# A two-layer hybrid attention encoder on one core: another order of each layer's projections, other waits between the planner's lines

## The chip, the cores and the metric

The kernel runs on one core of a Trainium2 chip. The time is the device time of one execution in microseconds (us). A core has five engines that run their own instruction streams and wait for each other by semaphores: TensorE (PE, matmuls; PEld is its loading of the stationary operand), VectorE (DVE), ScalarE (ACT), GpSimd (POOL) and SyncE (SP, which here only issues DMA transfers). DMA transfers can also be issued from ACT's and POOL's instruction streams. A line number such as L241 is one of the kernel before.

## What is computed

Two layers, each one RMSNorm, one wide input projection, two kinds of attention side by side, gates, an output projection and a residual add; then a final RMSNorm. The sequence has 512 positions, the model 1024 features, all in float32.

```python
for layer in range(DEPTH):                               # 2
    h = rms_norm(x, norm_g[layer])
    p = h @ w_in[layer]
    c_q, c_kv, k_r, gate_a, dil_qkv, gate_b = jnp.split(p, split_points, axis=-1)
    a = mla_attention(c_q, c_kv, k_r, q_norm_g[layer], kv_norm_g[layer],
                      w_uq[layer], w_ukv[layer], cos_m, sin_m) * jax.nn.silu(gate_a)
    b = dilated_attention(dil_qkv, cos_d, sin_d) * jax.nn.silu(gate_b)
    x = x + jnp.concatenate([a, b], axis=-1) @ w_out[layer]
return rms_norm(x, final_g)
```

`mla_attention` is latent attention: queries, keys and values of 8 heads come from two normed low-rank latents (`c_q` with 384 features, `c_kv` with 256), and a shared rotated key joins them. `dilated_attention` has three groups of 8 heads of width 64 with windows (128, 512, 2048) and key strides (1, 4, 16); the three groups' outputs are mixed per position by their softmax denominators.

## The kernel before

Every float32 operand is kept as a high and a low half (`hl`, `whl` and so on), and every product is three matmuls into one PSUM bank, high by high, high by low and low by high (`triple`, L241 to L243). A weight tile is loaded by SP into `wraw`; ACT rounds it to the high half (L198); the low half is either a VectorE subtraction (L203) or, for the kinds in `ADDED` that come after place `FROM` in the plan, a negation by ACT (L200) and an adding DMA from POOL's queue (L201).

The order of the work is not written out. Each piece is a generator task. One main line holds a layer's projections in the order of the table `ORDER` and behind them the output projection (`wp`, `wq`, `wo` in layer 0, `wa` to `wj` in layer 1). The names in `ORDER`: `ckv` and `cq` the two latents, `v` the values of the wide windows, `nv` those of the narrow window, `mv` and `muk` the latent attention's values and keys, `muq` and `mur` its queries and their rotated part, `kr` the shared key, `dqk u 0` and `dqk u 1` the queries and keys of window unit u (12 units of two heads, numbered so that four pairs of heads go through the three windows), `ga` and `gb` the gates of the two branches. Beside the main line run side lines, each strictly in its own order: `nline` (norms: `norm`, `lckv`, `lcq`), `sline` (scores), `tline` (outputs, named `o`) and `cline` (combining and gating: `mo` gates a pair of latent heads, `do1` mixes the three windows of a pair, `do` gates them). `Weave` walks the main line with a clock of its own and lets a side task start when all it needs was done a given lag earlier; only when the main line is blocked by a need are side tasks forced ahead of their lags. The lags of before are LAG 2.5 for norms and combining, LM 2.0 for latent scores, LD 8.25 (LD0 10.0 for the first) for window scores, LG 6.0 and LG2 16.5 for outputs behind their scores. A side task is placed in the order of its line, so a late task holds up those behind it on its line. What comes out is then given to a tile scheduler and to pools with fixed numbers of buffers: 8 PSUM banks, 4 `whl`, 14 `hl`, 2 `xl`, 8 `p`, 5 `v`, 5 `tmp`.

The places that the steps below touch:

- **Start** (L286 to L298): ACT's queue issues the first weight tile, the norm factors `gn` (L289) and the second weight tile; SP's queue the inputs and the other six tiles. PE runs WARM matmuls on zeros (L296). Each input tile is scaled by `gn` and split (`take_x`, L273 and L274) and enters the first latent products (L376).
- **Query latent**: each chunk is squared (L350) and the squares are added by POOL (L354 for `cq`); PE turns the sum (L256), and the norm factor goes into every query (L491).
- **Rotated queries** `mla_rope`: L497 on VectorE, L498 on POOL, L499 and L500 on VectorE, a split; `mla_query` copies them into each head's `q` on POOL (L512). The latent scores are L241 to L243 on `kml` and `q`, with the maximum on VectorE (L525).
- **Window scores**: narrow window L673 with L680 on VectorE, wide windows L744 and L747 with L750 and L753. **Outputs**: probabilities are turned by PE (L449), split by ACT and VectorE (L221, L222) and multiplied by the values: L550 for latent heads, L785 for wide windows. L785 gives four banks a unit, each summed by ACT (L788) and VectorE (L789, L791).
- **Mixing** `combine`: PE turns the shares (L819), ACT copies them (L821), SP writes them to DRAM (L822) and reads them back spread over partitions by four transfers (L827); VectorE scales two windows' outputs (L831), POOL adds them (L832). `combine_last` adds the third on VectorE (L837), gates (L433) and splits (L221, L222).
- **Output projection** of layer 0: each 128 features of the next x are one bank; `out_add` loads x (L844), adds (L845), writes the sum to DRAM (L846) and hands it on to the next layer's `take_x`, through two `xl` buffers. Layer 1 ends with the final norm (L913 to L926) and the output writes.

A window score task of before waits for the unit's values as well as for its queries and keys:

```python
att.append((i, ("d", u), [k("dqk", u, 0), k("dqk", u, 1), k("v", g, p // 2) if g else k("nv", p)],
            far_scores if g else near_scores, far_out if g else near_out))
```

Of the kernel before, what the change touches and what calls it, by code (L numbers as in the profile page):

```python
# [22 lines left out]
AHEAD, RATE, LAG, CAP = 3, 451.1, 2.5, 34.9  # L23
STEP, LD0, WARM, LG2, LY = 2, 10.0, 11, 16.5, 5.0
LV = 3.0
LG, LP, LD, LM, LC, LN, LX, LF = 6.0, 0.25, 8.25, 2.0, 14.25, 5.75, 5.0, 0.25
SHUF = [i + 8 if i < 8 else i - 8 if i < 16 else i for i in range(32)]

def forward_order():
    return [('ckv',), ('v', 1, 0), ('cq', 2), ('cq', 0), ('cq', 1), ('dqk', 0, 0), ('dqk', 0, 1), ('nv', 0), ('mur', 0), ('ga', 0), ('dqk', 1, 0), ('kr',), ('dqk', 1, 1), ('nv', 1), ('muq', 0), ('muk', 0), ('mv', 0), ('muq', 1), ('dqk', 2, 1), ('muk', 1), ('dqk', 2, 0), ('muq', 2), ('dqk', 3, 1), ('muq', 3), ('dqk', 3, 0), ('dqk', 4, 1), ('mur', 1), ('v', 2, 0), ('muq', 4), ('dqk', 4, 0), ('dqk', 5, 0), ('muk', 2), ('ga', 1), ('muq', 5), ('dqk', 5, 1), ('mv', 1), ('dqk', 6, 0), ('nv', 2), ('gb', 0), ('muq', 6), ('dqk', 6, 1), ('muq', 7), ('nv', 3), ('dqk', 8, 0), ('gb', 1), ('muk', 3), ('v', 1, 1), ('ga', 2), ('dqk', 7, 0), ('dqk', 7, 1), ('dqk', 10, 0), ('dqk', 8, 1), ('dqk', 9, 0), ('dqk', 9, 1), ('v', 2, 1), ('dqk', 10, 1), ('ga', 3), ('dqk', 11, 0), ('dqk', 11, 1), ('gb', 2), ('gb', 3)]  # L30


def unit(u):

    return u % 6 // 2, 2 * (u // 6) + u % 2
# [20 lines left out]
PLAN = PLANS[0]  # L56
ADDED = ("dqk", "nv", "ga", "gb")
FROM = PLAN.index(("dqk", 0, 1, 1))
# [79 lines left out]
def hybrid_encoder(ctx, tc, xT, wst, gains, fgain, tables, keytab, masks, out):  # L138
    nc = tc.nc
# [35 lines left out]
    gn = const.tile([128, 2 * NG], F32, name="gn")  # L175
# [112 lines left out]
    load_w(nc.scalar, 0)  # L288
    nc.scalar.dma_start(gn, gains)  # L289
    load_w(nc.scalar, 1)  # L290
# [641 lines left out]
    main, nline, sline, tline, cline = ([] for _ in range(5))  # L932
    for L in layers:
        l = L.l
        L.wo, L.x, L.acc, L.o = {}, [], {}, {}
        k = lambda *a: (l,) + a
# [5 lines left out]
        task(nline, k("lcq"), later(*[k("cq", c) for c in range(3)], k("norm")), latent_norm, "cq")  # L942
        for o in ORDER:
# [20 lines left out]
            else:  # L964
                u, qk = a
# [3 lines left out]
        for hd in range(8):  # L969
            p = hd // 2  # L970
            att.append((at["muq", hd], ("m", hd), [k("muq", hd), k("mv", hd // 4), k("muk", p), k("kr")], mla_scores, mla_head))
            if hd % 2:
                att.append((max(at["ga", p], at["muq", hd]) + 0.5, ("mo", p), later(k("ga", p), k("o", "m", hd)), None, mla_out))
        for u in range(12):
            g, p = unit(u)
            i = at["dqk", u, 1]
            att.append((i, ("d", u), [k("dqk", u, 0), k("dqk", u, 1), k("v", g, p // 2) if g else k("nv", p)],
                        far_scores if g else near_scores, far_out if g else near_out))
# [8 lines left out]
        for _, (what, n), needs, scores, f in sorted(att, key=lambda x: x[0]):  # L987
            if scores:
                task(sline, k("s0", what, n), [(x, LM if what == "m" else LD0 if n == 0 else LD) for x in needs], scores, n, 0)
                task(sline, k("s", what, n), now(*before[0]), scores, n, 1)  # L990
                task(tline, k("o", what, n), [(k("s", what, n), LG2 if what == "d" and unit(n)[0] == 2 else LG)], f, n)
                before = [before[1], [("t", l, what, n)]]
            else:
                task(cline, k(what, n), needs, f, n)
# [3 lines left out]
        if last:  # L998
            at = [i for i, x in enumerate(main) if x[0] == k("gb", 2)][0]
# [27 lines left out]
    Weave(RATE, CAP).run(main, [nline, sline, tline, cline])  # L1027
# [115 lines left out]
```

## Time and profile before

| | |
|---|---|
| Time, median of 3 runs (lowest to highest) | 928.56 us (927.87 to 929.92) |
| Profiled execution: its own time | 929.99 us |
| its span | 928.2 us |
| mean granted TensorE clock | 0.996 |
| DMA | 118.14 MB, mean 127 GB/s |

The span runs from the first to the last instruction that the profiler recorded, so 1.8 us of the execution's time lie around it. In a row of the timeline stand the start and the duration in us, the engine, the line, the operation, and its output and inputs by their names in the program. A matmul's recorded end is modelled and matmuls overlap in the pipe, so the distance of two starts says more of PE's pace than one duration. In a list of groups a row has the count, the summed busy time in us, the mean of one in ns, and the idle time of the engine ahead of the group with what ended it. DVEq, ACTq, POOLq and SPq are those engines' instruction queues, among others where they issue DMAs.

### The profile page before, as it was taken

The page shows a single profiled execution, that of the slowest core. Times are in us where ns is not written, and L with a number is a line of the kernel's source. Part 1 is how long each engine was busy: PE and PEld are TensorE (multiplying, and loading weights), DVE is VectorE, ACT ScalarE, POOL GpSimd, SP SyncE. Part 2 cuts the span into 40 slices and gives each one's busy share as a digit, 9 for nine tenths or more (in the row PEclk, how much of TensorE's full clock was granted, in tenths as well). Part 3 has the DMA queues.
Part 4 walks back from the last instruction along what each step waited for, and adds up shares of the span by engine and source line. Part 5 has one row for each costly group of instructions (what it writes and reads, how often), then busy time and mean ns, then how long its engine had stood idle before and what let it go on. Part 6 is the DMA issues. An engine that isn't in the chain of part 4 may idle for free.

```text
span 928.2 us, 15855 instructions
## 1 busy us (share of the span) xinstructions
PE 908.0 (98%) x5175; PEld 773.4 (83%) x5175; DVE 692.4 (75%) x1733; ACT 597.6 (64%) x1449; POOL 313.2 (34%) x365
## 2 busy tenths in 40 slices
PE   9999999999999999999999999999999999999996
PEld 7978888988889889887897888889888888898785
DVE  6756787877868776688766679787878676767964
ACT  6546876667757766764445468756768586676533
POOL 0134253345542432233211343524464234224300
PEclk9999999999999999999999999999999999999998
DMA  8457453276554764664453653615667558367542
GB/s 271 121 124 146 97 123 69 65 163 148 122 124 93 148 125 107 137 155 132 166 169 95 146 121 82 126 40 134 138 126 158 129 101 167 78 142 138 147 125 91
DMA packets 86466, 118.14 MB, mean 127 GB/s; under 512 B 16944, under 2 KB 37232, under 8 KB 86384
## 3 DMA queue, kind: packets, MB, share of 16 engines
q1 hardware_dynamic: 66656, 81.59, 30.6%
q0 software_dynamic: 19296, 35.14, 24.0%
q8 instruction: 41, 0.67, 0.3%
q10 hardware_dynamic: 432, 0.41, 0.1%
q14 instruction: 41, 0.34, 0.1%
HBM read 112.74 MB, written 4.36 MB: 126 GB/s over the span
## 4 chain that ended last, share of the span: by engine, by line
PE 83%; DVE 8%; ACT 4%; issue 2%; DMA 1%; POOL 1%; ACTq 0%; DVEq 0%; POOLq 0%
PE bank L241 22%; PE bank L242 22%; PE bank L243 22%; PE bank L449 5%; PE bank L550 3%; PE bank L376 3%; PE bank L744 1%; PE bank L785 1%; PE bank L673 1%; DVE pt L222 1%; DVE whl L203 1%; ACT whl L198 1%; DMA p<-wst 1%; DMA wraw<-wst 1%; DVE tmp L630 1%
## 5 line engine op out<-in xcount | busy, mean ns | idle before, releaser
L241 PE MATMUL bank<-hl,whl 128*128 128x512 f32 x712 | 283.9, 399 | 2.2 <-ACT hl L221 1.3
L242 PE MATMUL bank<-hl,whl 128*128 128x512 f32 x712 | 278.3, 391 | 0.0
L243 PE MATMUL bank<-hl,whl 128*128 128x512 f32 x712 | 278.1, 391 | 0.0
L198 ACT CAST whl<-wraw 128x512 fp32r<-128x512 f32 (+3 forms) x243 | 143.8, 596 | 121.2 <-PE bank L243 80.2
L201 POOL DMA_DIRECT2D whl<-wst x134 | 117.9, 884 | 225.2 <-ACT whl L200 152.7
L243 PEld LDWEIGHTS bank<-hl,whl 128*128 128x128 f32 x712 | 133.6, 188 | 29.5 <-DMA whl<-wst 0.4
L241 PEld LDWEIGHTS bank<-hl,whl 128*128 128x128 f32 x712 | 133.7, 188 | 28.5 <-ACT hl L221 1.7
L242 PEld LDWEIGHTS bank<-hl,whl 128*128 128x128 f32 x712 | 134.0, 188 | 23.9 <-DVE hl L222 0.3
L241 PE MATMUL bank<-whl,hl 128*128 128x256 f32 (+2 forms) x328 | 99.6, 304 | 1.6 <-ACT hl L221 1.6
L243 PE MATMUL bank<-whl,hl 128*128 128x256 f32 (+2 forms) x328 | 97.9, 298 | 0.0
L242 PE MATMUL bank<-whl,hl 128*128 128x256 f32 (+2 forms) x328 | 97.7, 298 | 0.0
L628 POOL TENSOR_TENSOR tmp<-tmp,sd 128x512 f32<-128x512 f32 x48 | 63.2, 1316 | 91.9 <-DVE tmp L626 65.4
L203 DVE TENSOR_TENSOR whl<-wraw,whl 128x512 fp32r<-128x512 f32 (+3 forms) x109 | 76.6, 710 | 23.1 <-ACT whl L198 22.1
L222 DVE TENSOR_TENSOR pt<-bank,pt 128x512 fp32r<-128x512 f32 x128 | 83.6, 684 | 5.4 <-ACT pt L221 4.0
L200 ACT ACTIVATE whl<-wraw 128x512 fp32r<-128x512 f32 x134 | 85.0, 634 | 0.1
L221 ACT CAST pt<-bank 128x512 fp32r<-128x512 f32 x128 | 69.9, 588 | 10.7 <-PE bank L449 10.3
L530 POOL TENSOR_SCALAR p<-p,lc 128x512 f32<-128x512 f32 x64 | 48.8, 769 | 70.0 <-DVE lc L529 64.2
L449 PE MATMUL bank<-ident,p 128*128 128x128 f32 x512 | 67.7, 275 | 0.0
L241 PEld LDWEIGHTS bank<-whl,hl 128*128 128x128 f32 x328 | 62.3, 190 | 3.9 <-ACT hl L221 1.8
L243 PEld LDWEIGHTS bank<-whl,hl 128*128 128x128 f32 x328 | 62.3, 190 | 2.0 <-DVE hl L222 0.4
L242 PEld LDWEIGHTS bank<-whl,hl 128*128 128x128 f32 x328 | 62.4, 190 | 1.7
L449 PEld LDWEIGHTS bank<-ident,p 128*128 128x128 f32 x512 | 59.2, 142 | 5.4
(181 smaller groups left out, 1620.1 us busy)
## 6 DMA issues: line engine op xcount, KB each, us to landing
wraw<-wst SPq DMA_DIRECT2D x218, 256.0 KB, 3.1
whl<-wst POOLq DMA_DIRECT2D x134, 256.0 KB, 4.4
tmp<-shd SPq DMA_DIRECT2D x32, 128.0 KB, 4.3
xl<-xT SPq DMA_DIRECT2D x10, 256.0 KB, 2.9
wraw<-wst SPq DMA_DIRECT2D x16, 144.0 KB, 2.3
wraw<-wst SPq DMA_DIRECT2D x12, 192.0 KB, 2.6
x1d<-xl SPq DMA_DIRECT2D x8, 256.0 KB, 3.2
xl<-x1d SPq DMA_DIRECT2D x8, 256.0 KB, 3.2
```

What stands on the lines that cost most here:

```text
L198: nc.scalar.copy(hi, src)
L200: nc.scalar.mul(lo, src, -1.0)
L201: nc.gpsimd.dma_start(lo, wst[emitted[0], :, :c], accum_op=ALU.add)
L203: nc.vector.tensor_tensor(lo, src, F(hi), op=ALU.subtract)
L221: nc.scalar.copy(dst_hi, src)
L222: nc.vector.tensor_tensor(dst_lo, src, F(dst_hi), op=ALU.subtract)
L241: nc.tensor.matmul(a, w[:, 0], h[:, 0], start=first, stop=False)
L242: nc.tensor.matmul(a, w[:, 0], h[:, 1], start=False, stop=False)
L243: nc.tensor.matmul(a, w[:, 1], h[:, 0], start=False, stop=last)
L449: nc.tensor.transpose(b[:, 128 * i:128 * i + 128], x, ident)
L530: nc.gpsimd.tensor_scalar(pt, pt, l1, 0.0, op0=ALU.mult, op1=ALU.add)
L628: nc.gpsimd.tensor_tensor(u, u, L.sd, op=ALU.mult)
```

## The change

- `ORDER` is another sequence of the same 61 projections.
- The query latent's norm `lcq` starts LQ = 5.0 after the three `cq` chunks instead of 2.5.
- Latent and window scores no longer need the values; the output task `o` needs them instead, LO = 4.0 after they are done.
- `mo`, the gating of latent outputs, gets a side line of its own, `gline`, instead of its place in `cline`.
- `gn` is loaded from GpSimd's queue instead of ACT's, and PE's warm-up has 10 matmuls instead of 11.
- `FROM` is the later of the first tiles' places of units' queries and keys in the plan, and `load_ahead` in layer 1 stands at the later of `gb 2` and `muq 7`, since their order is now another one.

The cut diff (of the table only the ends of the two lines, where the last eight entries are):

```diff
-STEP, LD0, WARM, LG2, LY = 2, 10.0, 11, 16.5, 5.0
-LV = 3.0
+STEP, LD0, WARM, LG2, LY = 2, 10.0, 10, 16.5, 5.0
+LV, LQ, LO = 3.0, 5.0, 4.0
...
-... ('dqk', 9, 0), ('dqk', 9, 1), ('v', 2, 1), ('dqk', 10, 1), ('ga', 3), ('dqk', 11, 0), ('dqk', 11, 1), ('gb', 2), ('gb', 3)]
+... ('v', 1, 1), ('muq', 7), ('dqk', 8, 1), ('dqk', 8, 0), ('v', 2, 1), ('dqk', 9, 1), ('dqk', 11, 0), ('dqk', 10, 1), ('gb', 3), ('dqk', 11, 1)]
...
-FROM = PLAN.index(("dqk", 0, 1, 1))
+FROM = max(PLAN.index(("dqk", 0, i, 1)) for i in range(2))
...
-    load_w(nc.scalar, 0)
-    nc.scalar.dma_start(gn, gains)
-    load_w(nc.scalar, 1)
+    nc.gpsimd.dma_start(gn, gains)
+    for k in range(2):
+        load_w(nc.scalar, k)
...
-        task(nline, k("lcq"), later(*[k("cq", c) for c in range(3)], k("norm")), latent_norm, "cq")
+        task(nline, k("lcq"), [(k("cq", c), LQ) for c in range(3)] + later(k("norm")), latent_norm, "cq")
...
-            att.append((at["muq", hd], ("m", hd), [k("muq", hd), k("mv", hd // 4), k("muk", p), k("kr")], mla_scores, mla_head))
+            att.append((at["muq", hd], ("m", hd), [k("muq", hd), k("muk", p), k("kr")], mla_scores, mla_head))
...
-            att.append((i, ("d", u), [k("dqk", u, 0), k("dqk", u, 1), k("v", g, p // 2) if g else k("nv", p)],
+            att.append((i, ("d", u), [k("dqk", u, 0), k("dqk", u, 1)],
...
-                task(tline, k("o", what, n), [(k("s", what, n), LG2 if what == "d" and unit(n)[0] == 2 else LG)], f, n)
+                g, p = unit(n) if what == "d" else (0, 0)
+                values = k("mv", n // 4) if what == "m" else k("v", g, p // 2) if g else k("nv", p)
+                task(tline, k("o", what, n), [(k("s", what, n), LG2 if g == 2 else LG), (values, LO)], f, n)
...
-                task(cline, k(what, n), needs, f, n)
+                task(gline if what == "mo" else cline, k(what, n), needs, f, n)
...
-            at = [i for i, x in enumerate(main) if x[0] == k("gb", 2)][0]
+            at = [i for i, x in enumerate(main) if x[0] in (k("gb", 2), k("muq", 7))][-1]
...
-    Weave(RATE, CAP).run(main, [nline, sline, tline, cline])
+    Weave(RATE, CAP).run(main, [nline, sline, tline, cline, gline])
```

In the old table `gb 2` and `gb 3` stand behind all window units; in the new one `gb 2` stands in the middle of the layer and `gb 3` ahead of the last unit's keys.

More of the change, by code (lines that the diff above doesn't have):

```diff
@@ L29, in forward_order @@
 def forward_order():
-    return [('ckv',), ('v', 1, 0), ('cq', 2), ('cq', 0), ('cq', 1), ('dqk', 0, 0), ('dqk', 0, 1), ('nv', 0), ('mur', 0), ('ga', 0), ('dqk', 1, 0), ('kr',), ('dqk', 1, 1), ('nv', 1), ('muq', 0), ('muk', 0), ('mv', 0), ('muq', 1), ('dqk', 2, 1), ('muk', 1), ('dqk', 2, 0), ('muq', 2), ('dqk', 3, 1), ('muq', 3), ('dqk', 3, 0), ('dqk', 4, 1), ('mur', 1), ('v', 2, 0), ('muq', 4), ('dqk', 4, 0), ('dqk', 5, 0), ('muk', 2), ('ga', 1), ('muq', 5), ('dqk', 5, 1), ('mv', 1), ('dqk', 6, 0), ('nv', 2), ('gb', 0), ('muq', 6), ('dqk', 6, 1), ('muq', 7), ('nv', 3), ('dqk', 8, 0), ('gb', 1), ('muk', 3), ('v', 1, 1), ('ga', 2), ('dqk', 7, 0), ('dqk', 7, 1), ('dqk', 10, 0), ('dqk', 8, 1), ('dqk', 9, 0), ('dqk', 9, 1), ('v', 2, 1), ('dqk', 10, 1), ('ga', 3), ('dqk', 11, 0), ('dqk', 11, 1), ('gb', 2), ('gb', 3)]
+    return [('ckv',), ('v', 1, 0), ('dqk', 0, 1), ('cq', 1), ('cq', 0), ('cq', 2), ('dqk', 0, 0), ('dqk', 1, 0), ('muk', 0), ('nv', 0), ('mur', 0), ('muq', 0), ('kr',), ('dqk', 1, 1), ('mv', 0), ('dqk', 2, 0), ('dqk', 2, 1), ('muq', 1), ('nv', 1), ('gb', 0), ('muq', 2), ('muk', 1), ('dqk', 3, 0), ('dqk', 3, 1), ('ga', 0), ('muq', 3), ('mur', 1), ('nv', 2), ('dqk', 7, 0), ('ga', 1), ('muk', 2), ('muq', 4), ('dqk', 4, 1), ('dqk', 5, 0), ('dqk', 4, 0), ('mv', 1), ('v', 2, 0), ('gb', 1), ('muq', 5), ('dqk', 5, 1), ('dqk', 6, 0), ('nv', 3), ('dqk', 6, 1), ('gb', 2), ('muk', 3), ('muq', 6), ('dqk', 10, 0), ('dqk', 9, 0), ('dqk', 7, 1), ('ga', 2), ('ga', 3), ('v', 1, 1), ('muq', 7), ('dqk', 8, 1), ('dqk', 8, 0), ('v', 2, 1), ('dqk', 9, 1), ('dqk', 11, 0), ('dqk', 10, 1), ('gb', 3), ('dqk', 11, 1)]
 def unit(u):
@@ L930, in out_sums @@
                 nc.sync.dma_start(rows[:, 512 * j + 256 * i:512 * j + 256 * i + 256], o[j][:, 256 * i:256 * i + 256])
-    main, nline, sline, tline, cline = ([] for _ in range(5))
+    main, nline, sline, tline, cline, gline = ([] for _ in range(6))
     for L in layers:
```

## The prediction

> **What bounds the kernel now.** I read the page first: the share of each engine and the chain that ended last.
>
> ```profile
> span 928.2 us, 15855 instructions
> PE 908.0 (98%) x5175; PEld 773.4 (83%) x5175; DVE 692.4 (75%) x1733; ACT 597.6 (64%) x1449; POOL 313.2 (34%) x365
> PE 83%; DVE 8%; ACT 4%; issue 2%; DMA 1%; POOL 1%; ACTq 0%; DVEq 0%; POOLq 0%
> ```
>
> TensorE is busy for 98% of the span and carries 83% of the chain. The change leaves every count as it was but for one warm-up matmul, so the work on PE stays. Only PE's idle time can be won, and only new idle time can lose. The waits of PE say where that idle time is (instruction that waited, releaser, total, times, longest):
>
> ```profile
> PE bank L241 <- ACT hl L221: 2.9, 2, 1.6
> PE bank L256 <- POOL tmp L354: 1.8, 2, 0.9
> PE bank L296 <- DVE q L293: 1.5, 1, 1.5
> PE bank L744 <- ACT q L221: 1.4, 2, 0.7
> PE bank L550 <- ACT pt L221: 1.2, 2, 0.6
> PE bank L747 <- DVE q L222: 1.1, 2, 0.5
> PE bank L550 <- DVE pt L222: 0.9, 2, 0.4
> PE bank L241 <- DVE st L680: 0.9, 1, 0.9
> PE bank L785 <- DVE og L791: 0.7, 2, 0.4
> PE bank L376 <- ACT hl L273: 0.6, 2, 0.3
> ```
>
> They add to 13.0 us, in three groups. The start of the program has 1.5 + 0.6 = 2.1. The end of each layer, where the last attention outputs meet the output projection, has 2.9 + 0.7 = 3.6 (one wait of each kind in either layer). The middle, where scores wait for their queries, outputs for their turned probabilities and the latent norm for its sum of squares, has 1.8 + 1.4 + 1.2 + 1.1 + 0.9 + 0.9 = 7.3. One more loss shows only in the windows (columns: PE, PEld, DVE, ACT and POOL busy, granted clock, DMA share, GB/s):
>
> ```profile
> 130.00:134.00 4.00, 3.02 (x23) 2.21 (x22) 3.91 (x7) 2.96 (x6) 3.14 (x3) 1.00 0.80 172
> 134.00:138.00 4.00, 4.00 (x24) 3.49 (x24) 3.37 (x14) 3.06 (x11) 0.90 (x1) 0.62 0.62 109
> 415.00:445.00 30.00, 28.45 (x136) 23.05 (x135) 26.02 (x57) 14.58 (x36) 9.25 (x10) 1.00 0.42 124
> 865.00:900.00 35.00, 32.95 (x174) 27.00 (x173) 29.25 (x69) 18.56 (x48) 8.47 (x10) 1.00 0.50 151
> ```
>
> At 130 to 134 us PE idled 0.98 us, in pieces, and in the next four microseconds the granted clock was 0.62: 0.38 x 4 = 1.5 us of matmul time lost. The other two rows are the layer ends: PE idle 1.55 and 2.05 us, and VectorE busy 87% and 84%, so there is little spare on it there.
>
> What a matmul of 512 columns costs I take from the timeline of PE, 15 matmuls apart: (418.10 - 414.69) / 15 = 0.227 us.
>
> ```profile
> 414.69 0.40 PE L243 MATMUL bank<-hl,whl 128*128 128x512 f32 x1
> ...
> 418.10 0.39 PE L243 MATMUL bank<-hl,whl 128*128 128x512 f32 x1
> ```
>
> **The middle: what goes.** L256 turns the sum of squares of the query latent once POOL has added the last chunk's square (L354). On PE, before (`bank_105` is that last chunk, `bank_117` the next projection):
>
> ```order
> L243 MATMUL bank_105_592<-hl_34_190,whl_100_554 128x512
> L241 MATMUL bank_117_648<-hl_20_148,whl_102_571 128x512
> ...
> L243 MATMUL bank_117_648<-hl_26_166,whl_102_571 128x512
> L256 MATMUL bank_122_668<-ident_66,tmp_57_321 128x128 x4
> L241 MATMUL bank_117_648<-hl_28_172,whl_107_595 128x512
> ```
>
> and now, with the lag LQ = 5.0 (`bank_118` is the last chunk):
>
> ```order
> L243 MATMUL bank_118_650<-hl_34_189,whl_108_597 128x512
> L241 MATMUL bank_125_692<-hl_20_147,whl_115_629 128x512
> ...
> L243 MATMUL bank_125_692<-hl_34_189,whl_120_653 128x512
> L256 MATMUL bank_136_741<-ident_66,tmp_57_320 128x128 x4
> L241 MATMUL bank_139_762<-hl_20_147,whl_122_670 128x512
> ```
>
> 12 matmuls of cover (2.7 us) became 24 (5.4). Needed are 2.7 + 0.9 = 3.6, so the wait of 0.9 goes in both layers, with 1.8 to spare. The first far scores (L744) stood 25 matmuls behind their query's projection and stand 92 behind it now; the waits of L744 and L747 go. The waits of L550 and the one behind L680 stood at places that the new order dissolves. Together 7.3 us; the clock loss, which follows such bubbles, 1.5; and each of some 11 restarts costs 0.1 more, since the first matmul after a wait passes at 0.32 instead of 0.227 (434.24 to 434.56 in these rows):
>
> ```profile
> 434.24 0.48 PE L241 MATMUL bank<-hl,hl 128*128 128x512 f32 x1
> 434.56 0.40 PE L242 MATMUL bank<-hl,hl 128*128 128x512 f32 x1
> ```
>
> That is 7.3 + 1.5 + 1.1 = **-9.9**, with ends -7.3 (clock and restarts lost elsewhere again) and -10.4 (some of the modelled matmul ends hide further idle time).
>
> On the clock the Trainium skill ("TensorE: Matmul & The Clock Gate", Part 1) says that the clock halves after an idle window of some 3.4 us. This trace does not agree: the clock fell behind gaps of under 1 us each. By the page none of my bubbles would cost clock and this term would be 1.5 smaller; the trace decides.
>
> **The middle: what comes.** The first latent (MLA) score L241 reads a rotated query: from the projection's bank through VectorE's L491, L497, L499, POOL's L498, VectorE's L500, a split on ACT and VectorE, and POOL's L512. Before, 211 PE instructions lie between bank and score, now 29, or 29 x 0.227 = 6.6 us. The rows:
>
> ```profile
> L498 POOL TENSOR_TENSOR tmp<-tmp,cms 128x512 f32<-128x512 f32 x4 | 5.8, 1461 | 8.5 <-DVE tmp L497 8.5
> L512 POOL TENSOR_SCALAR q<-mr 32x1024 fp32r<-32x1024 f32 x16 | 18.0, 1124 | 9.0 <-DVE mr L222 7.7 <-PE bank L747 0.3
> L222 DVE TENSOR_TENSOR pt<-bank,pt 128x512 fp32r<-128x512 f32 x128 | 83.6, 684 | 5.4 <-ACT pt L221 4.0
> L789 DVE TENSOR_TENSOR tmp<-bank,tmp 64x256 f32<-64x256 f32 x64 | 26.9, 420 | 10.6 <-ACT tmp L788 9.6
> L791 DVE TENSOR_TENSOR og<-bank,tmp 64x256 f32<-64x256 f32 x64 | 26.9, 420 | 1.7
> ```
>
> give 1.46 + 1.12 + five steps of 0.68 = 6.0, and two or three unrelated VectorE steps stand between, so 0 to 2 us are missing. I take 0.9, the size of the nearest row (L256 on POOL's L354), in each layer, and 0.3 for one far score pair that the order now splits: **+2.1**, ends +1 and +4.
>
> **The end of layer 0.** The last window unit's outputs (L785) are summed by L789 and L791 before a bank comes free. Before, on PE:
>
> ```order
> L243 MATMUL bank_938_5067<-hl_683_3650,hl_946_5108 128x512
> L785 MATMUL bank_960_5173<-pt_948_5122,v_806_4389 128x256 x2
> L785 MATMUL bank_962_5180<-pt_948_5122,v_806_4389 128x256 x2
> L785 MATMUL bank_964_5187<-pt_950_5130,v_806_4389 128x256 x2
> L241 MATMUL bank_915_4962<-hl_954_5147,hl_926_5009 128x512
> ```
>
> Their transposes (L449) stood 20 rows earlier, with 18 projection matmuls between. Now:
>
> ```order
> L785 MATMUL bank_945_5121<-pt_926_5027,v_805_4382 128x256 x2
> L785 MATMUL bank_947_5128<-pt_926_5027,v_805_4382 128x256 x2
> L449 MATMUL bank_949_5135<-ident_66,p_906_4921 128x128 x4
> L449 MATMUL bank_951_5143<-ident_66,p_911_4949 128x128 x4
> L785 MATMUL bank_954_5152<-pt_950_5140,v_806_4383 128x256 x2
> L785 MATMUL bank_956_5159<-pt_950_5140,v_806_4383 128x256 x2
> L785 MATMUL bank_958_5166<-pt_952_5148,v_806_4383 128x256 x2
> L785 MATMUL bank_960_5173<-pt_952_5148,v_806_4383 128x256 x2
> L241 MATMUL bank_962_5180<-hl_406_2131,whl_935_5075 128x512
> ```
>
> Nothing lies between, and five of the eight banks hold open sums, so three rotate: `bank_962` is that of `bank_956`. Ahead of it VectorE has four pairs L789 and L791 (4 x 0.84), two splits (2 x 0.68), one gating step of about 0.7, and ACT's first copy about 0.4: 5.8 us. PE has twelve half-width matmuls and eight transposes, some 2.2 us by halves and quarters of 0.227 with restarts. Stall 5.8 - 2.2 = 3.6, ends 1.4 and 4.5.
>
> Then the last gated output (the `do` of pair 3, `hl_972` in both). Its shares go through DRAM:
>
> ```profile
> 424.63 0.27 PE L819 MATMUL bank<-ident,e 128*24 128x128 f32 x1
> 425.54 0.33 SPq L822 DMA_DIRECT2D shd<-ku  x1
> 427.92 2.56 SPq L827 DMA_DIRECT2D tmp<-shd  x4
> 434.56 0.68 DVE L831 TENSOR_TENSOR og<-og,tmp 128x512 f32<-128x512 f32 x1
> 435.32 1.68 POOL L832 TENSOR_TENSOR og<-og,og 128x512 f32<-128x512 f32 x1 [8.38 <-DVE og L831]
> 437.08 0.68 DVE L222 TENSOR_TENSOR hl<-tmp,hl 128x512 fp32r<-128x512 f32 x1
> 445.39 1.23 PE L241 MATMUL bank<-hl,hl 128*128 128x512 f32 x4
> ```
>
> From L819 to the split's end is 437.76 - 424.63 = 13.1 us in this instance; with VectorE fuller I allow 14. PE's first use came 20.8 after L819. Now (`hl_966` is pair 2):
>
> ```order
> L243 MATMUL bank_962_5180<-hl_853_4661,whl_935_5075 128x512
> L819 MATMUL bank_967_5204<-ident_66,e_915_4972 24x128
> L241 MATMUL bank_888_4841<-hl_966_5201,hl_903_4899 128x512
> ...
> L243 MATMUL bank_1001_5375<-hl_522_2798,whl_989_5305 128x512
> L241 MATMUL bank_888_4841<-hl_972_5221,hl_903_4899 128x512
> ```
>
> 51 matmuls lie between: 51 x 0.227 = 11.6 us against 13.1 to 14: stall 2.0 (1.5 to 4). From there to the next layer's first L376 stood 76 PE instructions (17.3 us), now 38 (8.6). Its inputs x go out and back through two buffers:
>
> ```profile
> x1d<-xl SPq DMA_DIRECT2D x8, 256.0 KB, 3.2
> xl<-x1d SPq DMA_DIRECT2D x8, 256.0 KB, 3.2
> ```
>
> A round of 6.4 per pair is still covered at 8.6, two in a row are not: 1.5 (0 to 3.4). The layer end in sum 3.6 + 2.0 + 1.5 = 7.1, against about 1.3 + 0.3 + 0.1 = 1.7 there now: **+5.4**, ends +2 and +9.
>
> **The end of layer 1.** The same reorder, but rows of other products stand between those L449 and L785, and 46 matmuls (10.4 us) between L819 and pair 3: 1.2 + 2.5 + 0.4 for a tighter tail = 4.1, against 1.6 + 0.4 + 0.4 = 2.4: **+1.7** (0 to +3.6).
>
> **The start.** The norm factors leave ACT's queue for POOL's.
>
> ```profile
> 0.74 0.20 POOL masks.py:197 MEMSET ident<- 128x128 f32 x1 [0.29 <-POOLq L1134]
> 1.18 0.46 ACTq L289 DMA_DIRECT2D gn<-gains x1
> 1.67 0.45 ACTq L287 DMA_DIRECT2D p<-wst  x1
> gn<-gains ACTq DMA_DIRECT2D x1, 13.0 KB, 4.3
> whl<-wst POOLq DMA_DIRECT2D x134, 256.0 KB, 4.4
> ```
>
> ACT's second weight load issues 0.49 earlier. On POOL the load of `gn` stands right behind the memset of `ident`: 0.74 + 0.20 + 4.4 = 5.3, against 1.18 + 4.3 = 5.5 now, so the first L376, which waits for it, starts 0.2 earlier, and its second wait shrinks. The other half of `ident` is pushed back by one DMA issue; the first transposes that read it come tens of microseconds later. One warm-up matmul less ends before anything is ready. Together **-0.3** (-0.5 to +0.4). The Trainium skill ("DMA: Bandwidth & Descriptors", Latency and other measured facts) gives GpSimd's queue a first byte some 0.4 us later than the hardware queues'; by it the term would be +0.1. The two rows, 0.1 apart, do not show that.
>
> **The sum** against the profiled execution's 929.99: -9.9 + 2.1 + 5.4 + 1.7 - 0.3 = -1.0. That execution is 1.43 above the median of three (928.56); I put the same difference on the median: **927.6**. 0.2% is 1.86 us, about what a measurement of this kernel can tell from no change: 926.7 to 930.4 is the same.
>
> **The rivals.**
> *The ends cost little* (32%): the planner's cover holds, because VectorE reaches the sums of the last unit early or DMA comes back fast. For it: the layer ends idled only 1.55 and 2.05 us at 87% and 84% of VectorE. Against: the rows above. The ends then cost +2 and +1, and the first scores +1: -9.9 + 1 + 2 + 1 - 0.3 = -6.2: 922.4, or 920 to 925.
> *The layer end decides* (23%, slower): with the last unit in a lump and L819 with half its cover, PE stops for several pieces of about 1 us one after another, and the clock follows as it did at 134 us. With ends of +9 and +3.6 and two clock losses of 1.5 this is -9.9 + 2.1 + 9 + 3.6 + 3.0 - 0.3 = +7.5 at the worst; two thirds of the way there from the forecast is +4.7: 933.2. It decides from ends that cost 10 us more together (10 - 8.1 is 0.2% of the time), against the forecast's 7.1.
> *The order does nothing that counts* (5%): the stalls move to other places of the same size: 928.6.
>
> **How the numbers follow.** My forecast has 40%, its own range 925.0 to 930.0. Faster by over 0.2%: 0.30 of the first rival and 0.12 of the forecast, 0.42. Slower: 0.20 of the second and 0.05 of the forecast, 0.25. Within: 0.33. The range 921.5 to 933.4 takes in some two thirds of the first rival and half of the second.
>
> **What would show it.** Right: in the waits of PE the lines L256, L744, L747 and L550 gone or under 0.3, no window of clock under 0.9 in the middle, and at the end of layer 0 L785 and L241 waiting on L791 and on `hl`'s split, 5 us or more together. Wrong: idle under 3 us in the 30 us around layer 0's last L819, or a clock under 0.9 there, or new waits in the middle over 4 us.

## The result and the profile after

The changed kernel takes 955.86 us (median of 4, 954.55 to 961.66) against 928.74 for the kernel before beside it: a ratio of 1.0303, 95% interval 1.0279 to 1.0327. The forecast was 927.6, its range ended at 933.4. The profiled execution is the slowest of the four, 961.66 with a span of 959.5, so its waits add to some 6 us more than the median has.

The page after has PE at 96% instead of 98%. Its chain that ended last could be followed back only to 486.4 us, so its shares add up to 48% and cannot be set beside the 83% of before:

```profile
span 959.5 us, 15844 instructions
PE 921.7 (96%) x5174; PEld 779.3 (81%) x5174; DVE 702.3 (73%) x1733; ACT 596.2 (62%) x1449; POOL 310.0 (32%) x366
PE 35%; issue 4%; DVE 4%; ACT 2%; POOL 2%; DMA 1%; POOLq 0%; DVEq 0%; ACTq 0%
```

The waits of PE after (columns as before):

```profile
PE bank L243 <- DMA whl<-wst: 3.9, 4, 1.6
PE bank L744 <- DVE kst L222: 3.6, 2, 1.9
PE bank L376 <- ACT hl L273: 3.5, 2, 3.2
PE bank L572 <- DVE tmp L564: 3.2, 2, 1.9
PE bank L241 <- POOL q L512: 3.0, 2, 1.5
PE bank L744 <- DVE st L753: 1.8, 1, 1.8
PE bank L449 <- DVE st L753: 1.6, 1, 1.6
...
PE bank L376 <- DVE hl L274: 1.3, 2, 0.9
...
```

Every wait of the middle that the prediction struck out is gone: L256, L744 and L747 on queries, L550. A new set stands in its place, and most of it was not in the prediction. By stage, before and after (idle PE is the width less the first busy figure). The second window holds the end of layer 0 in both: layer 1's first L376 on its new input starts at 463.4 us before and at 485.2 after. The last window ends with the last product.

```profile
20.00:395.00 375.00, 370.94 (x2189) 319.42 (x2188) 278.64 (x720) 252.09 (x622) 134.97 (x154) 1.00 0.56 120
395.00:505.00 110.00, 108.45 (x555) 90.76 (x554) 84.80 (x185) 56.91 (x126) 30.13 (x35) 1.00 0.50 146
505.00:865.00 360.00, 356.83 (x2102) 305.26 (x2102) 273.05 (x693) 245.36 (x602) 138.91 (x160) 1.00 0.57 121
865.00:921.00 56.00, 53.82 (x269) 43.93 (x267) 40.30 (x105) 26.73 (x70) 8.47 (x10) 1.00 0.41 127
```

```profile
20.00:395.00 375.00, 369.16 (x2164) 315.80 (x2163) 275.17 (x684) 245.24 (x593) 136.07 (x155) 1.00 0.56 121
290.00:294.00 4.00, 4.00 (x20) 3.14 (x17) 2.12 (x11) 3.60 (x15) 0.00 (x0) 0.57 0.96 170
395.00:505.00 110.00, 98.27 (x479) 80.90 (x479) 78.45 (x180) 51.77 (x129) 23.34 (x29) 0.94 0.40 119
505.00:865.00 360.00, 355.36 (x2065) 302.71 (x2064) 266.32 (x647) 238.41 (x573) 132.94 (x151) 1.00 0.55 121
562.00:567.00 5.00, 5.00 (x19) 4.22 (x20) 2.52 (x5) 2.52 (x6) 2.52 (x3) 0.66 0.88 197
865.00:951.00 86.00, 80.70 (x406) 65.45 (x404) 63.98 (x183) 43.36 (x124) 16.18 (x24) 0.96 0.36 96
```

Idle PE went from 4.1 to 5.8 us in the middle of layer 0, from 1.6 to 11.7 at its end, from 3.2 to 4.6 in the middle of layer 1 and from 2.2 to 5.3 at its end. On top the clock took 0.06 x 110 = 6.6 us at the first end, 0.04 x 86 = 3.4 at the second, and 1.7 at each of the two places of 290 and 562 us, against 1.5 in one place before. So the ends hold about 23 of some 28 us that these windows show, and the middle, which should have given 8, cost 5.

### The profile page after: what moved, and what is told of

It is laid out like the page before. It is cut to its first block, busy times and chain, and to the rows that moved or that the text cites. A ratio compares the mean times of both kernels' runs of the same rounds, so it can differ in the third digit from the quotient of the medians.

```text
span 959.5 us, 15844 instructions
## 1 busy us (share of the span) xinstructions
PE 921.7 (96%) x5174; PEld 779.3 (81%) x5174; DVE 702.3 (73%) x1733; ACT 596.2 (62%) x1449; POOL 310.0 (32%) x366
## 5 line engine op out<-in xcount | busy, mean ns | idle before, releaser
L241 PE MATMUL bank<-hl,whl 128*128 128x512 f32 x712 | 290.0, 407 | 0.0
L243 PE MATMUL bank<-hl,whl 128*128 128x512 f32 x712 | 280.9, 395 | 3.9 <-DMA whl<-wst 3.9
L242 PE MATMUL bank<-hl,whl 128*128 128x512 f32 x712 | 280.7, 394 | 0.0
L201 POOL DMA_DIRECT2D whl<-wst x134 | 116.8, 874 | 256.2 <-ACT whl L200 158.9
L243 PEld LDWEIGHTS bank<-hl,whl 128*128 128x128 f32 x712 | 135.3, 190 | 35.4 <-DMA whl<-wst 5.7
L241 PEld LDWEIGHTS bank<-hl,whl 128*128 128x128 f32 x712 | 135.6, 190 | 26.4 <-issue 0.2
L242 PEld LDWEIGHTS bank<-hl,whl 128*128 128x128 f32 x712 | 135.9, 191 | 22.8
L241 PE MATMUL bank<-whl,hl 128*128 128x256 f32 (+2 forms) x328 | 99.8, 304 | 1.3 <-ACT hl L221 1.3
L243 PE MATMUL bank<-whl,hl 128*128 128x256 f32 (+2 forms) x328 | 98.0, 299 | 0.0
L203 DVE TENSOR_TENSOR whl<-wraw,whl 128x512 fp32r<-128x512 f32 (+3 forms) x109 | 82.2, 757 | 21.3 <-ACT whl L198 20.6
L200 ACT ACTIVATE whl<-wraw 128x512 fp32r<-128x512 f32 x134 | 85.0, 634 | 0.1
L528 ACT ACTIVATE p<-bank,nm 128x512 f32<-128x512 f32 x64 | 43.8, 687 | 39.0 <-DVE nm L525 38.0
L530 POOL TENSOR_SCALAR p<-p,lc 128x512 f32<-128x512 f32 x64 | 50.1, 794 | 54.9 <-DVE lc L529 54.3
L241 PEld LDWEIGHTS bank<-whl,hl 128*128 128x128 f32 x328 | 62.2, 190 | 3.9 <-ACT hl L221 2.0
L243 PEld LDWEIGHTS bank<-whl,hl 128*128 128x128 f32 x328 | 62.2, 190 | 2.1 <-DVE hl L222 0.6
```

Source lines behind the costliest of these rows:

```text
L200: nc.scalar.mul(lo, src, -1.0)
L201: nc.gpsimd.dma_start(lo, wst[emitted[0], :, :c], accum_op=ALU.add)
L203: nc.vector.tensor_tensor(lo, src, F(hi), op=ALU.subtract)
L241: nc.tensor.matmul(a, w[:, 0], h[:, 0], start=first, stop=False)
L242: nc.tensor.matmul(a, w[:, 0], h[:, 1], start=False, stop=False)
L243: nc.tensor.matmul(a, w[:, 1], h[:, 0], start=False, stop=last)
```

## The experiments

Each kernel was timed in three rounds (the last two in five) against the kernel before on the same chip; a ratio is to that kernel, with its 95% interval.

### Table or rules?

The new table alone on the old rules has no order at all: unit 2's keys wait for unit 1's scores, and those for the values `nv 1`, which stand behind these keys in the new table. So the rules were tried with the old table.

```diff
-    return [... the new table]
+    return [... the old table]
```

> The old table of projections with all other edits of the change kept (scores without values, LO, LQ, gline, gn on GpSimd's queue, 10 warm-up matmuls). Theory T (the loss is the new table's): 926 to 932 us, the waits L744 on kst gone, no clock under 0.9 at the layer ends. Rival R (the loss comes from the new rules between the planner's lines, since scores run without values and outputs heap up): 945 us or more. Either way the layer boundary's L376 wait under 0.5 us if T.

Measured: 942.59, ratio 1.0148 (1.013 to 1.0166). It lies between the theories: the rules cost 13.5 us by themselves, the table 13.3 on top. Neither theory holds alone. The windows of its two ends:

```profile
395.00:505.00 110.00, 107.47 (x550) 89.71 (x549) 86.46 (x187) 57.08 (x128) 28.09 (x35) 1.00 0.50 145
865.00:932.00 67.00, 61.63 (x314) 50.34 (x313) 46.76 (x121) 30.14 (x76) 8.46 (x12) 1.00 0.42 123
```

Its layer 0 end is nearly whole (idle 2.5 us), so that end is the table's. Its layer 1 end idles 5.4 us, as much as the changed kernel's 5.3 though in other waits (L785 and a low half), but at the full clock: what the table adds there is the lost clock.

### What in the table: keys, buffers or the order of the last third?

Two kernels went after single waits that the changed kernel shows at the ends, a third after the order of its last entries.

```diff
-    kst = const.tile([128, 2, S], FR, name="kst")
+    ksts = [const.tile([128, 2, S], FR, name=f"kst{i}") for i in range(2)]
...
-                task(main, k(*o), now(k("s", "d", u - 1)) if qk and u else [], dil_qk, u, qk)
+                task(main, k(*o), now(k("s", "d", u - 2)) if qk and u > 1 else [], dil_qk, u, qk)
```

> The changed kernel with a second buffer for a unit's keys, so a unit's key projection needs the scores of the unit before the last, not of the last. Theory K (in the new table's end the key projections of units 8 to 11 lie one projection apart, and the single key buffer forces the scores of units 9 and 10 straight behind their keys): the waits L744 on kst (3.6 us) and L744 on L753 (1.8) go, with the clock lost behind them (two places of about 1.7 in layer 0, one of 3.4 in layer 1): 10 to 13 us less than the changed kernel, 943 to 946. Rival (VectorE is simply too full there and is late whatever the key buffer): less than 4 us gained.

Measured: 965.78, ratio 1.0393 (1.0371 to 1.0414). Theory K falls: the kernel is slower than the changed one, by some 9 us. The wait for the keys shrank to 0.7 us, and others grew:

```profile
PE bank L572 <- DVE tmp L564: 5.2, 2, 2.6
PE bank L787 <- DVE og L793: 3.1, 3, 1.7
PE bank L746 <- DVE og L793: 3.0, 1, 3.0
```

(Lines here are two further on: L746 is the score of before's L744, L787 its L785, L793 its L791.) The last row is a score that waits for a bank which the outputs' sums hold.

```diff
-        return t([128, S], F32, "xl", 2)
+        return t([128, S], F32, "xl", 4)
```

> The changed kernel with four xl buffers instead of two. Theory X (the waits of L376 at the layer boundary, 3.2 and 1.3 us, and the clock of 0.5 to 0.68 behind the first come from the round of x through two buffers): 4.5 to 7 us less, 949 to 951, the wait of L376 on L273 under 0.5. Rival (the bank or VectorE is what L845 waits for): within 1.5 us of the changed kernel.

Measured: 956.61, ratio 1.0291 (1.0275 to 1.0308), as the changed kernel. The waits of L376 for x fell from 4.8 to 0.5 us as theory X says, and the time did not: L376 now waits 2.0 us for a weight's low half, L744 for its keys 4.1 instead of 3.6, and L572, in the middle of the layers, 5.2 instead of 3.2. Taking away one wait moved the idle time to others.

The third kernel set the last entries of the table anew.

```diff
-... ('ga', 2), ('ga', 3), ('v', 1, 1), ('muq', 7), ('dqk', 8, 1), ('dqk', 8, 0), ('v', 2, 1), ('dqk', 9, 1), ('dqk', 11, 0), ('dqk', 10, 1), ('gb', 3), ('dqk', 11, 1)]
+... ('ga', 2), ('v', 1, 1), ('muq', 7), ('dqk', 8, 1), ('dqk', 8, 0), ('dqk', 9, 1), ('v', 2, 1), ('dqk', 10, 1), ('ga', 3), ('dqk', 11, 0), ('dqk', 11, 1), ('gb', 3)]
```

> The changed kernel with the last entries of the table set as the old table has them: the values of the third window between the keys of units 9 and 10, two gates around the last unit, gate 3 last. Theory K: two or more projections lie between successive keys again and more main work lies behind the last unit, so 14 to 20 us are won back, 936 to 942. Rival R (rules): under 5 us. It leaves the layer boundary of two xl buffers: 0 to 5 us of that may stay.

Measured: 962.21, ratio 1.0367 (1.0321 to 1.0413), a miss. The end of layer 0 did improve (idle 9.4 instead of 11.7, clock 0.98 instead of 0.94), but I had left unit 8's queries directly ahead of unit 9's keys, so unit 8's scores were forced straight behind their own queries, and L744 waited 5.4 us for those. The run says little of the question; the next one asks it properly.

```diff
-... ('muk', 3), ('muq', 6), ('dqk', 10, 0), ('dqk', 9, 0), ('dqk', 7, 1), ('ga', 2), ... ('gb', 3), ('dqk', 11, 1)]
+... ('muk', 3), ('muq', 6), ('muq', 7), ('dqk', 8, 0), ('v', 1, 1), ('ga', 2), ('dqk', 7, 1), ('dqk', 10, 0), ('dqk', 8, 1), ('dqk', 9, 0), ('dqk', 9, 1), ('v', 2, 1), ('dqk', 10, 1), ('ga', 3), ('dqk', 11, 0), ('dqk', 11, 1), ('gb', 2), ('gb', 3)]
```

> The changed kernel whose table keeps the new order up to the sixth query and takes the old order of what is left, with gates 2 and 3 behind all window units. Theory C (of the 27 us, the table's part comes from its end: two projections behind unit 10's keys and none behind unit 11's, where the old table has five and two, so that the chain scores, outputs, mixing, projection, next x has nothing beside it): the layer ends fall from 11.7 and 5.0 us of idle PE to 3 and 5, no clock under 0.9 at layer 0's end, 940 to 945 as with the whole old table. Rival M (the new table's middle costs as much): 948 or more.

Measured: 944.32, ratio 1.0167 (1.0147 to 1.0187): theory C holds. The last third (18 of the 61 entries; only `muk 3` still stands earlier than in the old table) is worth 11.5 of the 13.3 us that the table costs. The 1.7 left for the rest cannot be told from nothing, since the interval overlaps that of the old table. The windows of the two ends:

```profile
395.00:505.00 110.00, 106.65 (x548) 89.20 (x547) 86.65 (x196) 56.63 (x134) 29.90 (x36) 1.00 0.50 144
865.00:936.00 71.00, 65.83 (x332) 53.62 (x331) 50.30 (x129) 32.56 (x81) 12.35 (x21) 1.00 0.43 122
```

Idle PE at layer 0's end is 3.4 us instead of 11.7, at the full clock; layer 1's end keeps its 5.2 us, which the old table didn't take away either. The same move was made the other way round in the kernel before:

```diff
-... ('ga', 3), ('dqk', 11, 0), ('dqk', 11, 1), ('gb', 2), ('gb', 3)]
+... ('ga', 3), ('gb', 2), ('dqk', 11, 0), ('gb', 3), ('dqk', 11, 1)]
```

> The kernel before with one move in its table: the last two gate projections stand ahead of unit 11's queries and keys instead of behind them, so that no projection lies behind the last keys (48 matmuls, 10.9 us, before). Theory C: 6 to 12 us slower than before, 936 to 942, all of it at the two layer ends. Rival: the ends' work is bound by VectorE, whose work is the same, so within 3 us of before.

Measured: 936.29, ratio 1.0088 (1.0058 to 1.0118), 6.9 us slower, inside what C expected, though only in layer 0:

```profile
395.00:505.00 110.00, 103.87 (x521) 86.78 (x520) 82.33 (x176) 53.15 (x119) 25.61 (x32) 0.98 0.49 140
865.00:926.00 61.00, 58.80 (x294) 47.70 (x293) 44.16 (x118) 27.81 (x71) 8.60 (x11) 1.00 0.39 118
```

6.1 us idle instead of 1.6 and 2.2 of clock at layer 0's end, 6.7 more together; at layer 1's end 2.2 idle as before. That layer 1's output projection has rows of earlier heads to put beside it may be why; no run shows that. So 48 matmuls of unrelated projections moved from behind the last unit's keys to ahead of them cost 7 us in a layer, with no instruction added.

### Is the clock a cost of its own?

Seven places of the changed kernel show a clock of 0.5 to 0.7 behind a gap. Ten matmuls without use fill the gap at two of them.

```diff
+                if (u, part, j, a) == (10, 0, 0, 0):
+                    for _ in range(10):
+                        nc.tensor.matmul(banks[0], L.fill[:, 0, 0:128], L.h[7][:, 0], start=True, stop=True)
```

> The changed kernel with ten matmuls that count for nothing put on PE ahead of unit 10's scores in both layers, where PE waits 1.7 and 1.9 us for the keys (the product goes into the scores' bank and is overwritten). Theory H (the clock falls because of such gaps): the ten take 2.3 us, 0.5 more than each gap, and the clock of 0.5 to 0.66 behind them (2 us in layer 0, 3.4 in layer 1) does not fall: 3 to 5 us less than the changed kernel's 956. Rival (the clock falls anyway a little later, or it follows the light matmuls themselves and not the gap): 0 to 2 us more.

Measured: 962.85, ratio 1.037 (1.0328 to 1.0412). The first half of theory H is right. Changed kernel, then filled gap:

```profile
404.00:410.00 6.00, 4.97 (x27) 4.19 (x28) 5.91 (x20) 3.85 (x13) 0.00 (x0) 0.72 0.47 118
880.00:888.00 8.00, 7.68 (x33) 6.39 (x34) 7.84 (x32) 4.33 (x16) 0.00 (x0) 0.57 0.29 75
```

```profile
404.00:410.00 6.00, 6.00 (x35) 5.12 (x34) 5.78 (x29) 4.55 (x19) 0.00 (x0) 1.00 0.16 44
880.00:888.00 8.00, 8.00 (x46) 6.83 (x45) 7.71 (x34) 6.67 (x24) 0.00 (x0) 1.00 0.25 69
418.00:428.00 10.00, 5.68 (x28) 4.12 (x27) 6.57 (x16) 5.04 (x10) 0.00 (x0) 0.73 0.69 223
896.00:906.00 10.00, 4.93 (x29) 3.86 (x30) 6.97 (x26) 3.45 (x11) 0.00 (x0) 0.72 0.61 165
```

With the gap filled the clock stays at 1.00. The second half is wrong: the time did not fall. PE idled at the next place instead, 4.3 and 5.1 us in the two lower rows, where the changed kernel idles 1.6 in each of these windows, and the clock fell there. Over the whole end of layer 0 nothing is won: 12.0 us idle at a clock of 0.94, against 11.7 at 0.94.

```profile
395.00:505.00 110.00, 98.03 (x483) 80.11 (x482) 79.00 (x178) 49.67 (x119) 23.60 (x29) 0.94 0.41 122
```

So at these ends the idle time and the clock of one gap can't be added up as its cost: what was filled came back further on. The median rose by 7 us, and these rows do not say why. They can't: the profiled execution is the fastest of this kernel's four, and that of the changed kernel its slowest. The ten matmuls also take 2.3 us and read the last weight tile, which holds its buffer longer; that was not separated.

### The rules one by one

```diff
-            att.append((at["muq", hd], ("m", hd), [k("muq", hd), k("mv", hd // 4), k("muk", p), k("kr")], mla_scores, mla_head))
+            att.append((at["muq", hd], ("m", hd), [k("muq", hd), k("muk", p), k("kr")], mla_scores, mla_head))
...
+                task(tline, k("o", what, n), [(k("s", what, n), LG2 if g == 2 else LG), (values, LO)], f, n)
```

> The kernel before with only one edit: scores no longer wait for values, outputs wait for them with LO = 4.0. Theory S (of the 13.5 us that the rules cost with the old table, this rule makes most: scores run earlier, their shares on GpSimd's queue stand ahead of the low halves of the weights, and PE's L243 waits for those): 937 to 943 us with two waits of L243 on the adding DMA of about 3 us. Rival G (the gating line, LQ and the head make it): within 3 us of before, 926 to 932.

Measured: 937.17, ratio 1.0082 (1.0055 to 1.011). One list of waits names the place, `PE bank L243 <- DMA whl<-wst`, 5.6 us in two pieces, and GpSimd's timeline shows why, first in the kernel before, then with the rule:

```profile
213.38 0.89 POOL L201 DMA_DIRECT2D whl<-wst  x1 [5.78 <-ACT whl L200]
214.36 3.83 POOL L765 TENSOR_SCALAR p<-p,e 128x128 f32<-128x128 f32 x8
218.13 0.81 POOL L201 DMA_DIRECT2D whl<-wst  x1
```

```profile
211.56 3.69 POOL L765 TENSOR_SCALAR p<-p,e 128x128 f32<-128x128 f32 x8 [6.30 <-ACT whl L198]
215.23 1.36 POOL L530 TENSOR_SCALAR p<-p,lc 128x512 f32<-128x512 f32 x2
216.54 1.73 POOL L201 DMA_DIRECT2D whl<-wst  x2
```

The scores came earlier in the plan, so the scaling of their probabilities (L765, eight steps, 3.7 us, and two of L530) slipped ahead of a weight's adding DMA in GpSimd's queue, and that DMA is issued 3 us later. The granted clock fell behind both pieces, so the profiled execution, with 940.9 the slowest of the four, shows more than the waits. To tell cause from place, weights were ordered one tile earlier, with the rule and, as its control, without:

```diff
-AHEAD, RATE, LAG, CAP = 3, 451.1, 2.5, 34.9
+AHEAD, RATE, LAG, CAP = 4, 451.1, 2.5, 34.9
...
-        return t([128, 2, 512], FR, "whl", 4)
+        return t([128, 2, 512], FR, "whl", 5)
```

> The scores rule alone on the kernel before (937.2 us), with weight tiles four ahead and a fifth buffer. Theory S (that rule costs 7.6 us because the shares' scaling on GpSimd's queue stands ahead of the adding DMAs of the weights, and L243 waits 5.6 us for them): the waits of L243 go and 5 us or more with them, 929 to 932. Rival (the adding DMA is only where the delay shows, VectorE's chain ahead of the shares is the cause and another wait takes the place): 935 or more.

> The kernel before with weight tiles four ahead and a fifth buffer, as the control of the first of these runs: its PE waits hold no adding DMA, so within 2 us of 929, unless loads and casts that come earlier push other work on ACT and VectorE back (then slower).

Measured: 935.09 (ratio 1.0059, 1.0039 to 1.0078) with the rule, 935.86 (1.0067, 1.0047 to 1.0088) without. The waits of L243 are gone. By its own bounds the run falls to the rival, but its control costs as much without the rule: with weights four ahead the rule adds nothing. That fits theory S, as far as such costs add. Four ahead costs 6.5 us by itself, where I had expected at most 2 unless earlier loads and casts get in the way: L241 waits 3.8 us for `hl`'s split instead of 2.9, L785 2.2 for its sums instead of 0.7. In the changed kernel the same edit was a miss as well:

> The changed kernel with weight tiles four ahead instead of three and a fifth buffer for them. Theory W (PE's waits on low halves of weights, 3.9 us, and the clock lost behind one of them, 1.8, come from adding DMAs that stand behind other work on GpSimd's queue): these waits go, 4 to 6 us less, 950 to 952, and nothing else changes. Rival: the adding DMAs are late by more than one tile, or their place is taken by others: within 2 us.

Measured: 960.73, ratio 1.0338 (1.0313 to 1.0362). No wait for a weight's DMA is left there, and others are longer: L572 waits 5.2 us instead of 3.2, as it did with four xl buffers, and L241 for L512 3.6 instead of 3.0.

The small rules together, then apart:

```diff
-                task(cline, k(what, n), needs, f, n)
+                task(gline if what == "mo" else cline, k(what, n), needs, f, n)
...
-        task(nline, k("lcq"), later(*[k("cq", c) for c in range(3)], k("norm")), latent_norm, "cq")
+        task(nline, k("lcq"), [(k("cq", c), LQ) for c in range(3)] + later(k("norm")), latent_norm, "cq")
...
+    nc.gpsimd.dma_start(gn, gains)
```

> The kernel before with the other rules alone: gline, LQ = 5.0, gn on GpSimd's queue with 10 warm-up matmuls; table and values rule as before. Theory S: 926 to 930 us, the wait of L256 on L354 gone (1.8 us) and nothing new. Rival G: 936 us or more.

Measured: 934.38, ratio 1.0049 (1.0034 to 1.0065): nearer to rival G, which I had not favoured, though short of its price (4.7 us instead of 6.3 or more). Then the gating line alone, and the other two without it:

> The kernel before with gline alone (the gating of the last latent pair is started 22 us earlier by the planner's clock). If it makes the 4.5 to 5.5 us between the two runs of the small edits: 933 to 936, with L242 waiting some 2 us on a VectorE low half and L785 on L791 at the end of layer 1. Rival (only together with lag and head): 927 to 930.

> The kernel before with LQ = 5.0, gn on GpSimd's queue and 10 warm-up matmuls, and nothing else. If the 4.5 us of the three small edits together come from the gating line alone: 926 to 929, with the wait of L256 gone (1.8) and no wait of 2 us at the end of layer 1. If from lag or head: 932 to 935 as before.

Measured: 933.54 (1.0048, 1.0032 to 1.0063) for the line, 928.78 (1.0, 0.9988 to 1.0012) for lag and start. The line is all of it. With the old table it starts the gating of the last latent pair earlier (L433 on VectorE at 389.8 us instead of 419.2 in layer 0). PE then idles 4.8 us at the end of layer 1 instead of 2.2, and its list has new waits for a VectorE low half and for the sums:

```profile
PE bank L785 <- DVE og L791: 2.7, 2, 2.2
PE bank L242 <- DVE whl L203: 2.3, 1, 2.3
```

In the changed kernel, with that one line of the diff undone, it makes no difference that can be told:

> The changed kernel with the gating of latent outputs back on cline. If the line of its own only shifts small steps: within 3 us of the changed kernel's 956. If it is what presses VectorE at the layer ends (gating done early, mixing late): 6 us or more less.

Measured: 955.80, ratio 1.0276 (1.0244 to 1.0307). So the parts need not add: scores rule 7.6, gating line 4.5 and lag with start 0 make 12 of the 13.5 us of the rules with the old table, and the same line costs nothing that shows in the new one.

### What is left of it

The lag took away the wait of L256 (1.8 us), and 1.6 us of L572 came in its place: the turning of narrow values stands behind the latent norm on the same line. It got a line of its own, with the new and with the old start of the program.

```diff
-                task(nline, k(*o), [(k("nva", *a), LV)], turn_values, a[0])
+                task(vline, k(*o), [(k("nva", *a), LV)], turn_values, a[0])
```

> The kernel before with LQ = 5.0, gn on GpSimd's queue, 10 warm-up matmuls, and the turning of narrow values (nv) on a line of its own, so that it isn't held up behind the later latent norm (with the lag alone L572 took over the 1.8 us of L256 as 1.6). If the lag's gain is real once nothing is behind it: the waits of L256 and L572 both gone, 926 to 928, 0.2 to 0.3% faster than before. Rival (some other wait takes it): within 1 us of 929.

> The same with gn back on ACT's queue and 11 warm-up matmuls: tells the start apart. If the start is worth 0.3 us as forecast: 0 to 0.5 more than the run with it.

Measured: 928.60 (ratio 0.9992, 0.9981 to 1.0003) with `gn` on GpSimd's queue, 927.54 (0.998, 0.9971 to 0.999) with the old start. L256 and L572 are both off the list of waits in both. The second is the one version of this study that beats both kernels, the one before by 0.2%; the first can't be told from the kernel before. The old start is 1.1 us faster in the medians, where 0 to 0.5 slower was expected. The intervals of the two overlap, so the size stays open; the traces bear out the sign (see the start, below).

## Why the prediction was wrong

**The middle, what goes (-9.9): right in its rows.** All six kinds of waits went, and no clock was lost at 134 us. The row shown for the price of a restart (434.24) stands behind transposes and not behind a wait, but behind a wait of the changed kernel the step is the same 0.33 us (262.69 to 263.02). But the lag shows how little a struck wait is worth by itself: with the old table its 1.8 us came back as 1.6 on L572.

**The middle, what comes (+2.1, ends 1 to 4): failed.** The score behind L512 waits 1.5 us in each layer, where 0.9 was forecast, the right mechanism mis-sized. Two places weren't in the sum: L243 on adding DMAs, 3.9 us, and L572, 3.2. With the two clock losses of 1.7 the term is some 13 instead of 2. The step that failed is that I listed what a moved score reads and not what the moved pieces put ahead of others in the engines' own queues. On GpSimd's queue the scores rule alone shows it, and the rows of L201 and L765 stood in the trace of before. In the changed kernel it can hold for some of the waits only: before the 1.1 us at 262.7 GpSimd had two scalings of L530 right ahead of its DMAs, but before the longest wait, 1.6 at 288.5, it had been idle:

```profile
282.26 0.89 POOL L201 DMA_DIRECT2D whl<-wst  x1 [2.50 <-ACT whl L200]
283.31 0.86 POOL L201 DMA_DIRECT2D whl<-wst  x1 [0.15 <-PE bank L449]
```

There ACT's negation L200 came late, and why is open. L572's two waits, at 271.7 and 749.1 us, stand behind VectorE: L564 comes there right behind a unit's score steps and shares (L753 to L810). In the changed kernel no run separated that.

**The end of layer 0 (+5.4, ends 2 to 9): failed, by 11.** Of its three pieces the lump of L785 was about right, 3.6 forecast; the timeline of PE after has the waits one after another:

```profile
446.97 0.63 PE L449 MATMUL bank<-ident,p 128*128 128x128 f32 x4 [1.29 <-DVE og L791]
448.06 0.74 PE L785 MATMUL bank<-pt,v 128*128 128x256 f32 x4 [0.46 <-DVE pt L222]
449.26 0.50 PE L785 MATMUL bank<-pt,v 128*128 128x256 f32 x2 [0.46 <-DVE pt L222]
450.59 0.77 PE L785 MATMUL bank<-pt,v 128*128 128x256 f32 x2 [0.82 <-DVE og L791]
```

3.0 us. The trip of the shares through DRAM, forecast at 2.0, cost 0.3: from L819 to L832 it took 8.3 us there (455.2 to 463.5) instead of 10.7. The round of x, forecast at 1.5 with an end of 3.4, cost 4.6:

```profile
485.23 4.34 PE L376 MATMUL bank<-hl,whl 128*128 128x512 f32 x12 [3.23 <-ACT hl L273]
494.80 1.65 PE L376 MATMUL bank<-hl,whl 128*128 128x512 f32 x6 [0.87 <-DVE hl L274]
496.92 0.74 PE L376 MATMUL bank<-hl,whl 128*128 128x512 f32 x2 [0.47 <-DVE hl L274]
```

What was missing is everything ahead of the lump: L744's waits for the keys of unit 10 and for unit 11's banks, 3.5 us, and the clock, 6.6. I had counted cover between two chosen instructions, not the projections behind the last units: two behind unit 10's keys instead of five, none behind unit 11's instead of two. That is the step that failed: the last third of the table proved to be 11.5 us of the 27, and one such move alone 6.9.

**The end of layer 1 (+1.7, ends 0 to 3.6): failed**, with 3.1 us more idle time, 3.4 of clock and 1.5 in the tail behind the last product. The idle time was put down to the new order, but the old table with the new rules has as much (5.4 us idle), and the gating line alone nearly (4.8), both in other waits than the changed kernel; the sum had no term for that line. In the changed kernel 5.6 us stay when the gating line is undone, so what makes its idle time there is open.

**The start (-0.3): failed, in its sign.** GpSimd issued the load of `gn` at 1.32 us and not at 0.94, and the first L376 began at 6.38 instead of 6.32. The idle time of the first 20 us is 1.75 against 2.07 in these two executions, but that is luck. The first cast L273, which waits for `gn`, starts at 5.57 to 6.16 us in the 12 traces with `gn` on GpSimd's queue and at 5.16 to 5.55 in the 7 with it on ACT's; the first L376 starts at 6.54 and 6.32 in the median. So the edit loses some 0.2 us there instead of winning 0.3, and the other value that the prediction names, +0.1, has the right sign.

**The rivals.** The slower rival, that the layer end decides, named the mechanism, with a clock that follows the gaps, but priced it at 933; it took single stalls for the cost, where the whole chain from the last scores to the next layer's first product was short of cover. The row that should have raised its chance was the sum's own: a gain of 9.9 from the middle, against an end for which every piece had been found worse. Two of the forecast's own signs of being wrong came: a clock under 0.9 near layer 0's last L819 at 455.2 us, and 10 us of new waits in the middle, where 4 were allowed:

```profile
450.00:454.00 4.00, 3.41 (x9) 2.86 (x10) 3.74 (x8) 1.20 (x3) 0.00 (x0) 0.57 0.02 6
```

Open stays why the ends lose more than their parts (two key buffers, four xl buffers and the filled gap each took a wait away and won nothing), beyond that the order of the table's last third decides it.

## What to carry to other kernels

In a kernel whose engine is 98% busy, a new order is priced at its thinnest place: count the unrelated work that stands behind the start of the last long chain of a stage, before and after, and not the cover of the waits that the edit is about. A wait that is struck out is a gain only if nothing else is due just behind it; take it out alone and look who waits next. When instructions move, read the queue of every engine that they pass, GpSimd's with its DMA issues too.

## What the runs showed of the hardware

The length of a gap does not settle whether TensorE's clock falls behind it. The old table with the new rules, and the scores rule alone, wait at the same place, L243 between wide matmuls, for a late adding DMA. Two stretches of four microseconds each, the one with the wait and the next, first with the old table and the new rules (a wait of 3.09 us), then with the scores rule alone (2.50 us):

```profile
219.00:223.00 4.00, 1.01 (x7) 0.58 (x5) 2.38 (x5) 2.47 (x6) 1.60 (x2) 1.00 1.02 192
223.00:227.00 4.00, 3.90 (x21) 3.32 (x22) 0.79 (x2) 1.48 (x3) 0.86 (x1) 1.00 1.14 256
```

```profile
219.00:223.00 4.00, 1.50 (x9) 0.96 (x8) 2.54 (x6) 2.47 (x6) 1.56 (x3) 1.00 0.99 191
223.00:227.00 4.00, 4.00 (x16) 3.48 (x15) 1.81 (x4) 1.17 (x2) 0.72 (x1) 0.57 1.15 240
```

The longer wait kept the full clock, the shorter one was followed by 0.57. In layer 1 it is the same again: 2.76 us without a loss, 3.08 with one. In the changed kernel gaps of 1.5 to 1.9 us were followed by four microseconds at 0.57 to 0.66, and its four executions have mean clocks of 0.984 to 0.991. As far as these runs tell, a gap's price in clock is a chance and not a constant. The Trainium skill ("TensorE: Matmul & The Clock Gate", Part 1) has a free-running window of about 3.4 us of activity; a window that starts anywhere beside the gap would fit such pairs, but no run here varied that. Filling two gaps kept the clock up there, and it fell behind the next ones.
